# Packed transposes, a GpSimd cast and a hand-written order in an adapted linear layer

## The chip, the cores and the metric

The kernel runs on one core of a Trainium2 chip. The core has a matrix engine (TensorE, PE in the profile, its weight loads PEld), a vector engine (VectorE, DVE), a scalar engine (ScalarE, ACT), a general engine (GpSimd, POOL) and a synchronisation engine (SyncE, SP) that here only issues loads. All transfers run on the core's 16 DMA engines. The metric is device time in microseconds (us): the median of repeated runs. A profile comes from one profiled execution, whose own time is given beside its span.

## The reference

A linear layer whose weight is adapted by a low-rank product and normalised by column. x has 16 x 2048 rows of 256 values, all in fp32.

```python
W_adapted = W + scale * (lora_A @ lora_B)            # 256 x 256, rank 16
W_norm = np.sqrt(np.sum(W_adapted ** 2, axis=0, keepdims=True) + 1e-8)
W_final = (W_adapted / W_norm) * m                   # m: one value for each column
y = x.reshape(-1, 256) @ W_final                     # 32768 x 256
```

## The kernel before

**Start.** W, lora_A, lora_B and m are loaded (L60 to L66), and a short chain computes `w_final`, the final weight in bf16, as two halves of 128 input rows (index `c` or `kc`; input row k = 128 c + p lies on partition p). The chain is: transpose lora_A (L86), broadcast m with a matmul (L91), the low-rank product (L97), the sum with W (L106), squares (L110), column sums by a matmul with ones (L115), square root (L119), reciprocal (L124), and the scaling (L126).

**Main loop.** x is worked through in 8 blocks of 4096 rows. A block is one load of 4 MB on SP's queue (L52), in which partition p receives 32 consecutive rows of 256 values. Five buffers hold blocks, so the sixth load waits until the first block's store has emptied its buffer. A block is cut into 8 chunks of 4 rows for each partition, that is 512 rows, and 64 chunks make up the whole. For each chunk:

- TensorE transposes eight 128x128 pieces in fp32 (L141) into a PSUM tile `xt_ps`, which takes two banks; there are two such tiles.
- VectorE copies the tile to SBUF as bf16, `xt_sb` (L147); there are six such buffers.
- TensorE multiplies (L152): eight matmuls, each with one 128x128 piece of `xt_sb` as the stationary operand and a half of `w_final`, 256 columns, as the moving one, into `y_ps` (two banks, two tiles).
- ScalarE copies `y_ps` back over the rows of x in the block's buffer (L159).

After the last chunk ScalarE's queue issues the block's store of 4 MB (L161), and the buffer is free once it has landed. Loads are on one DMA queue (q1) and stores on the other (q10); both use the same 16 engines.

**Order.** The order on each engine is chosen by a planner from the program's order and its own costs; the start chain has a raised priority (L80). In the profile a number of transposes of later chunks are seen between the matmuls of earlier ones.

Of the kernel before, what the change touches and what calls it, by code (L numbers as in the profile page):

```python
# [10 lines left out]
@with_exitstack  # L11
def kernel(
    ctx: ExitStack,
    tc: tile.TileContext,
    x: bass.AP,
    W: bass.AP,
    lora_A: bass.AP,
    lora_B: bass.AP,
    m: bass.AP,
    scale: float,  # L20
    out: bass.AP,
):
    nc = tc.nc
    P = 128
    FP32 = mybir.dt.float32
    BF16 = mybir.dt.bfloat16
    AF = mybir.ActivationFunctionType
    ALU = mybir.AluOpType

    x_flat = x.flatten_outer_dims()  # L30
    out_flat = out.flatten_outer_dims()
    N, IN = x_flat.shape
    OUT = W.shape[1]
    R = lora_A.shape[1]
    KC = IN // P
    J = 4
    DJ = 32
    BLK = DJ * P
    NBLK = N // BLK

    assert IN == OUT and IN % P == 0 and OUT % P == 0 and N % BLK == 0

    consts = ctx.enter_context(tc.tile_pool(name="consts", bufs=1))
    startup = ctx.enter_context(tc.tile_pool(name="startup", bufs=1))
    xpool = ctx.enter_context(tc.tile_pool(name="xpool", bufs=5))
    xtpool = ctx.enter_context(tc.tile_pool(name="xtpool", bufs=6))
    pp_xt = ctx.enter_context(tc.tile_pool(name="pp_xt", bufs=2, space=bass.MemoryType.PSUM))
    pp_y = ctx.enter_context(tc.tile_pool(name="pp_y", bufs=2, space=bass.MemoryType.PSUM))

    def load_x(b):  # L50
        t = xpool.tile([P, DJ, IN], FP32, name="x_sb", tag="x_sb")
        nc.sync.dma_start(  # L52
            out=t,
            in_=x_flat[b * BLK : (b + 1) * BLK].rearrange("(p j) k -> p j k", p=P),
        )
        return t


    a_nat = startup.tile([P, KC, R], FP32)
    nc.scalar.dma_start(out=a_nat, in_=lora_A.rearrange("(c p) r -> p c r", p=P))  # L60
    w_nat = startup.tile([P, KC, OUT], FP32)
    nc.sync.dma_start(out=w_nat, in_=W.rearrange("(c p) o -> p c o", p=P))
    b_nat = startup.tile([R, OUT], FP32)
    nc.scalar.dma_start(out=b_nat, in_=lora_B)  # L64
    m_row = startup.tile([1, OUT], FP32)
    nc.scalar.dma_start(out=m_row, in_=m[None, :])  # L66

    identity = consts.tile([P, P], FP32)
    make_identity(nc, identity)
    ones = consts.tile([P, P], FP32)  # L70
    nc.vector.memset(ones, 1.0)
    eps_col = startup.tile([P, 1], FP32)
    nc.vector.memset(eps_col, 1e-8)

    warm = startup.tile([P, 1], FP32)
    nc.scalar.activation(out=warm, in_=eps_col, func=AF.Sqrt)  # L76

    w_final = consts.tile([P, KC, OUT], BF16)

    with tc.high_priority():  # L80
        b_bf = startup.tile([R, OUT], BF16)
        nc.vector.tensor_copy(out=b_bf, in_=b_nat)  # L82

        aT_ps = pp_y.tile([R, KC * P], FP32, tag="psy", name="aT_ps")
        for c in range(KC):
            nc.tensor.transpose(aT_ps[:, c * P : (c + 1) * P], a_nat[:, c, :], identity)  # L86
        aT = startup.tile([R, KC * P], BF16)
        nc.vector.tensor_copy(out=aT, in_=aT_ps)

        mb_ps = pp_y.tile([P, OUT], FP32, tag="psy", name="mb_ps")  # L90
        nc.tensor.matmul(mb_ps, ones[0:1, :], m_row, start=True, stop=True)  # L91
        m_all = startup.tile([P, OUT], FP32)
        nc.vector.tensor_copy(out=m_all, in_=mb_ps)  # L93

        ab_ps = pp_y.tile([P, KC, OUT], FP32, tag="psy", name="ab_ps")
        for c in range(KC):
            nc.tensor.matmul(  # L97
                ab_ps[:, c, :],
                aT[:, c * P : (c + 1) * P],
                b_bf,  # L100
                start=True,
                stop=True,
            )

        wa = startup.tile([P, KC, OUT], FP32)
        nc.vector.scalar_tensor_tensor(  # L106
            out=wa, in0=ab_ps, scalar=float(scale), in1=w_nat, op0=ALU.mult, op1=ALU.add
        )
        sq = startup.tile([P, KC, OUT], FP32)
        nc.vector.tensor_mul(out=sq, in0=wa, in1=wa)  # L110


        n2_ps = pp_y.tile([P, OUT], FP32, tag="psy", name="n2_ps")
        for c in range(KC):
            nc.tensor.matmul(  # L115
                n2_ps, ones, sq[:, c, :], start=(c == 0), stop=(c == KC - 1)
            )
        norm = startup.tile([P, OUT], FP32)
        nc.scalar.activation(out=norm, in_=n2_ps, func=AF.Sqrt, bias=eps_col)  # L119
        wam = startup.tile([P, KC, OUT], FP32)  # L120
        for c in range(KC):
            nc.vector.tensor_mul(out=wam[:, c], in0=wa[:, c], in1=m_all)  # L122
        rnorm = startup.tile([P, OUT], FP32)
        nc.vector.reciprocal(out=rnorm, in_=norm)  # L124
        for c in range(KC):
            nc.vector.tensor_mul(out=w_final[:, c], in0=wam[:, c], in1=rnorm)  # L126

    j_order = []
    for a in range(J // 2):
        j_order.append(a)  # L130
        j_order.append(a + J // 2)

    for b in range(NBLK):
        x_sb = load_x(b)


        for c in range(DJ // J):
            xt_ps = pp_xt.tile([P, KC, J * P], FP32, tag="psxt", name="xt_ps")
            for j in range(J):
                for kc in range(KC):  # L140
                    nc.tensor.transpose(  # L141
                        xt_ps[:, kc, j * P : (j + 1) * P],
                        x_sb[:, c * J + j, kc * P : (kc + 1) * P],
                        identity,
                    )
            xt_sb = xtpool.tile([P, KC, J * P], BF16, name="xt_sb")
            nc.vector.tensor_copy(out=xt_sb, in_=xt_ps)  # L147

            y_ps = pp_y.tile([P, J, OUT], FP32, tag="psy", name="y_ps")
            for kc in range(KC):  # L150
                for j in j_order:
                    nc.tensor.matmul(  # L152
                        y_ps[:, j, :],
                        xt_sb[:, kc, j * P : (j + 1) * P],
                        w_final[:, kc, :],
                        start=(kc == 0 and (j % (J // 2)) == 0),
                        stop=(kc == KC - 1 and (j % (J // 2)) == (J // 2) - 1),
                    )
            nc.scalar.copy(out=x_sb[:, c * J : (c + 1) * J, :], in_=y_ps)  # L159

        nc.scalar.dma_start(  # L161
            out=out_flat[b * BLK : (b + 1) * BLK].rearrange("(p j) k -> p j k", p=P),
            in_=x_sb,
        )


# [33 lines left out]
```

## Time and profile before

| | us |
|---|---|
| median of 11 runs (166.6 to 169.64) | 167.29 |
| profiled execution | 167.39 |
| its span, first to last instruction | 165.6 |
| TensorE matmul busy / weight loads | 129.3 / 108.2 |
| VectorE busy | 81.2 |
| ScalarE busy | 65.6 |
| GpSimd busy | 0.7 |
| block 0 lands | 13.9 |
| first store issued | 34.02 |
| last store issued | 153.39 |

67.55 MB are moved, at a mean of 408 GB/s over the span. The mean granted clock of TensorE is 0.973 of full speed.

How to read the lines: in the table of slices each digit is the busy share of a fortieth of the span in tenths. A group line gives the source line, the engine, the operation, output and input tiles with their shapes, the number of instructions, then busy us and the mean ns of one, then the idle time of the engine just before them and what ended most of it. Matmuls are pipelined, so the mean duration of one is longer than the spacing between two. The rows of stretches give, for a window of the span, each engine's busy time with its number of instructions, then the granted clock, the share of DMA and GB/s.

### The profile page before, as it was taken

To read this page: it belongs to the slowest core of one execution; us is meant where nothing else is said; L and a number is where in the kernel's file an instruction comes from. 1 tells how busy PE (TensorE), PEld (TensorE's weight loads), DVE (VectorE), ACT (ScalarE), POOL (GpSimd) and SP (SyncE) were. 2 spreads that over 40 slices of the span, in tenths; PEclk is the share of its full clock that TensorE was granted. 3 is DMA by queue.
4 is the path that set the end of the run, shared out by engine and by line. 5 is a ranking of instruction groups with operands and counts; after the bars stand their busy time and mean duration, and the time that the engine had idled before them with its cause. 6 is when DMAs were issued, how large, how long until landed. Compare 5 with 4: busy or idle time off the path is not lost.

```text
span 165.6 us, 2364 instructions
## 1 busy us (share of the span) xinstructions
PE 129.3 (78%) x1034; PEld 108.2 (65%) x1034; DVE 81.2 (49%) x76; ACT 65.6 (40%) x67; POOL 0.7 (0%) x6
## 2 busy tenths in 40 slices
PE   0149788888999889988998999889998699797000
PEld 0028677776788768876877778777786678685000
DVE  0155655558850895059553951577519350780000
ACT  3001244442068405960097039620780089329000
POOL 1000000000000000000000000000000000000000
PEclk9999999999999999999999999999999999999955
DMA  6999999999998999999999998999999999991885
GB/s 194 416 475 388 491 388 423 451 388 380 435 447 380 483 404 463 421 404 467 400 459 412 435 447 380 491 398 455 427 396 475 396 455 419 451 435 75 380 380 253
DMA packets 2892, 67.55 MB, mean 408 GB/s; under 512 B 561, under 2 KB 834, under 8 KB 834
## 3 DMA queue, kind: packets, MB, share of 16 engines
q1 hardware_dynamic: 1424, 33.82, 48.3%
q10 hardware_dynamic: 1458, 33.59, 47.3%
q8 instruction: 8, 0.13, 0.3%
q14 instruction: 2, 0.02, 0.0%
HBM read 33.85 MB, written 33.55 MB: 407 GB/s over the span
## 4 chain that ended last, share of the span: by engine, by line
PE 57%; DVE 22%; ACT 6%; DMA 4%; issue 2%; ACTq 1%
PE y_ps L152 32%; PE xt_ps L141 23%; DVE xt_sb L147 20%; ACT x_sb L159 6%; DMA m_row<-in_m_dram 4%; PE n_ps L115 1%; DVE rnorm L124 1%; PE mb_ps L91 1%; DVE w_final L126 0%; DVE sq L110 0%; DVE wa L106 0%; ACTq L60 0%; ACTq L64 0%; ACT norm L119 0%; PE ab_ps L97 0%
## 5 line engine op out<-in xcount | busy, mean ns | idle before, releaser
L147 DVE CAST xt_sb<-xt_ps 128x1024 bf16<-128x1024 f32 x64 | 75.5, 1219 | 55.8 <-PE xt_ps L141 41.8
L159 ACT COPY x_sb<-y_ps 128x1024 f32<-128x1024 f32 x64 | 63.6, 1014 | 75.2 <-PE y_ps L152 72.9
L141 PE MATMUL xt_ps<-identity,x_sb 128*128 128x128 f32 x512 | 71.3, 280 | 7.1 <-DVE xt_sb L147 6.5
L152 PE MATMUL y_ps<-w_final,xt_sb 128*128 128x256 bf16 x512 | 64.7, 272 | 6.1 <-DVE xt_sb L147 4.3
L141 PEld LDWEIGHTS xt_ps<-identity,x_sb 128*128 128x128 f32 x512 | 57.9, 143 | 15.9 <-DVE xt_sb L147 14.8
L152 PEld LDWEIGHTS <-xt_sb 128*128 128x128 bf16 x512 | 49.2, 97 | 16.7 <-DVE xt_sb L147 6.2
L119 ACT ACTIVATE norm<-n_ps,eps_col 128x256 f32<-128x256 f32 x1 | 0.5, 474 | 10.3 <-PE n_ps L115 10.3
L91 PE MATMUL mb_ps<-m_row,ones 1*128 1x256 f32 x2 | 1.2, 696 | 4.3 <-DMA m_row<-in_m_dram 4.3
L86 PE MATMUL aT_ps<-identity,a_nat 128*16 128x128 f32 x2 | 0.6, 394 | 4.0 <-DMA a_nat<-in_lora_A_dram 4.0
L91 PEld LDWEIGHTS mb_ps<-m_row,ones 1*128 1x128 f32 x2 | 0.5, 308 | 4.8 <-issue 4.8
L115 PE MATMUL n_ps<-sq,ones 128*128 128x256 f32 x4 | 2.1, 674 | 1.5 <-DVE sq L110 1.5
L82 DVE CAST b_bf<-b_nat 16x256 bf16<-16x256 f32 x1 | 0.3, 280 | 5.6 <-DMA b_nat<-in_lora_B_dram 5.6
L124 DVE RECIPROCAL rnorm<-norm 128x256 f32<-128x256 f32 x1 | 1.8, 1753 | 2.0 <-ACT norm L119 2.0
L86 PEld LDWEIGHTS aT_ps<-identity,a_nat 128*16 128x16 f32 x2 | 0.1, 88 | 4.0 <-issue 4.0
L115 PEld LDWEIGHTS n_ps<-sq,ones 128*128 128x128 f32 x4 | 1.2, 323 | 2.2 <-DVE sq L110 2.0
L76 ACT ACT_TABLE_LOAD x1 | 1.3, 1283 | 2.3 <-issue 2.3
L93 DVE COPY m_all<-mb_ps 128x256 f32<-128x256 f32 x1 | 0.4, 425 | 2.9 <-PE mb_ps L91 2.9
L126 DVE TENSOR_TENSOR w_final<-wam,rnorm 128x256 bf16<-128x256 f32 x2 | 0.8, 422 | 0.0
L122 DVE TENSOR_TENSOR wam<-wa,m_all 128x256 f32<-128x256 f32 x2 | 0.8, 416 | 0.0
L110 DVE TENSOR_TENSOR sq<-wa 128x512 f32<-128x512 f32 x1 | 0.7, 691 | 0.0
L106 DVE SCALAR_TENSOR_TENSOR wa<-ab_ps,w_nat 128x512 f32<-128x512 f32 x1 | 0.7, 691 | 0.0
L97 PE MATMUL ab_ps<-b_bf,aT 16*128 16x256 bf16 x2 | 0.6, 416 | 0.0
(11 smaller groups left out, 2.0 us busy)
## 6 DMA issues: line engine op xcount, KB each, us to landing
x_sb<-in_x_dram SPq DMA_DIRECT2D x8, 4096.0 KB, 31.3
out_dram<-x_sb ACTq DMA_DIRECT2D x8, 4096.0 KB, 25.7
w_nat<-in_W_dram SPq DMA_DIRECT2D x1, 256.0 KB, 3.0
a_nat<-in_lora_A_dram ACTq DMA_DIRECT2D x1, 16.0 KB, 3.1
b_nat<-in_lora_B_dram ACTq DMA_DIRECT2D x1, 16.0 KB, 5.3
m_row<-in_m_dram ACTq DMA_DIRECT2D x1, 1.0 KB
```

The source lines that it names most:

```text
L76: nc.scalar.activation(out=warm, in_=eps_col, func=AF.Sqrt)
L86: nc.tensor.transpose(aT_ps[:, c * P : (c + 1) * P], a_nat[:, c, :], identity)
L91: nc.tensor.matmul(mb_ps, ones[0:1, :], m_row, start=True, stop=True)
L106: nc.vector.scalar_tensor_tensor(out=wa, in0=ab_ps, scalar=float(scale), in1=w_nat, op0=ALU.mult, op1=ALU.add)
L115: nc.tensor.matmul(n2_ps, ones, sq[:, c, :], start=(c == 0), stop=(c == KC - 1))
L122: nc.vector.tensor_mul(out=wam[:, c], in0=wa[:, c], in1=m_all)
L124: nc.vector.reciprocal(out=rnorm, in_=norm)
L126: nc.vector.tensor_mul(out=w_final[:, c], in0=wam[:, c], in1=rnorm)
L141: nc.tensor.transpose(xt_ps[:, kc, j * P : (j + 1) * P], x_sb[:, c * J + j, kc * P : (kc + 1) * P], identity,)
L147: nc.vector.tensor_copy(out=xt_sb, in_=xt_ps)
L152: nc.tensor.matmul(y_ps[:, j, :], xt_sb[:, kc, j * P : (j + 1) * P], w_final[:, kc, :], start=(kc == 0 and (j % (J // 2)) == 0), stop=(kc ...
L159: nc.scalar.copy(out=x_sb[:, c * J : (c + 1) * J, :], in_=y_ps)
```

## The change

Four things change together.

1. **What is transposed.** GpSimd first casts a chunk of x to bf16 (`xb`, three buffers). Two neighbouring bf16 values of a row make up one 4-byte word, which is handed to TensorE as if it were one fp32 value. A row of 256 values is 128 words, so four transposes cover a chunk instead of eight. Partition p of the result holds input rows 2p and 2p+1 next to each other, for each of the 512 rows.
2. **What follows from it.** VectorE's copy out of PSUM moves 512 words instead of casting 1024 values. The result `xt` has three buffers; its PSUM tile takes one bank, and there are four. The stationary operand of a matmul is now every second bf16 value of `xt`. W and lora_A are loaded so that partition p holds input rows 2p and 2p+1 (index `t`), which matches.
3. **Order.** The planner is turned off and instructions stay in written order. The first five loads are written ahead of the start chain, later ones after the store that frees their buffer. The broadcast of m is written after the square root. Each chunk's cast, transposes and copy are written ahead of the matmuls of the chunk before; at the end of a block it is the other way round.
4. **Names.** The two halves of the loop become functions.

The stores stay one of 4 MB for each block.

```diff
-    xpool = ctx.enter_context(tc.tile_pool(name="xpool", bufs=5))
-    xtpool = ctx.enter_context(tc.tile_pool(name="xtpool", bufs=6))
-    pp_xt = ctx.enter_context(tc.tile_pool(name="pp_xt", bufs=2, space=bass.MemoryType.PSUM))
+    xpool = ctx.enter_context(tc.tile_pool(name="xpool", bufs=XBUFS))
+    xbpool = ctx.enter_context(tc.tile_pool(name="xbpool", bufs=3))
+    xtpool = ctx.enter_context(tc.tile_pool(name="xtpool", bufs=3))
+    pp_xt = ctx.enter_context(tc.tile_pool(name="pp_xt", bufs=4, space=bass.MemoryType.PSUM))
     pp_y = ctx.enter_context(tc.tile_pool(name="pp_y", bufs=2, space=bass.MemoryType.PSUM))
+    ctx.enter_context(tc.manual_schedule())
...
-    nc.scalar.dma_start(out=a_nat, in_=lora_A.rearrange("(c p) r -> p c r", p=P))
+    nc.scalar.dma_start(out=a_nat, in_=lora_A.rearrange("(p t) r -> p t r", t=KC))
     w_nat = startup.tile([P, KC, OUT], FP32)
-    nc.sync.dma_start(out=w_nat, in_=W.rearrange("(c p) o -> p c o", p=P))
+    nc.sync.dma_start(out=w_nat, in_=W.rearrange("(p t) o -> p t o", t=KC))
...
+    for b in range(XBUFS):
+        load_x(b)
...
-        mb_ps = pp_y.tile([P, OUT], FP32, tag="psy", name="mb_ps")
-        nc.tensor.matmul(mb_ps, ones[0:1, :], m_row, start=True, stop=True)
-        m_all = startup.tile([P, OUT], FP32)
-        nc.vector.tensor_copy(out=m_all, in_=mb_ps)
...
+    nc.scalar.activation(out=norm, in_=n2_ps, func=AF.Sqrt, bias=eps_col)
+
+    mb_ps = pp_y.tile([P, OUT], FP32, tag="psy", name="mb_ps")
+    nc.tensor.matmul(mb_ps, ones[0:1, :], m_row, start=True, stop=True)
+    m_all = startup.tile([P, OUT], FP32)
+    nc.vector.tensor_copy(out=m_all, in_=mb_ps)
...
-            for j in range(J):
-                for kc in range(KC):
-                    nc.tensor.transpose(
-                        xt_ps[:, kc, j * P : (j + 1) * P],
-                        x_sb[:, c * J + j, kc * P : (kc + 1) * P],
-                        identity,
-                    )
-            xt_sb = xtpool.tile([P, KC, J * P], BF16, name="xt_sb")
-            nc.vector.tensor_copy(out=xt_sb, in_=xt_ps)
...
+    def transposed(g):
+        b, c = divmod(g, CH)
+        rows = x_tiles[b][:, c * J : (c + 1) * J, :]
+        xb = xbpool.tile([P, J, IN], BF16, name="xb")
+        nc.gpsimd.tensor_copy(out=xb, in_=rows)
+        xt_ps = pp_xt.tile([P, J * P], FP32, tag="psxt", name="xt_ps")
+        for j in range(J):
+            nc.tensor.transpose(
+                xt_ps[:, j * P : (j + 1) * P], xb[:, j, :].bitcast(FP32), identity
+            )
+        xt = xtpool.tile([P, J * P, KC], BF16, name="xt")
+        nc.vector.tensor_copy(
+            out=xt.rearrange("p r t -> p (r t)").bitcast(FP32), in_=xt_ps
         )
+        xts[g] = xt
+
+    def multiplied(g):
...
+                nc.tensor.matmul(
+                    y_ps[:, j, :],
+                    xt[:, j * P : (j + 1) * P, t],
+                    w_final[:, t, :],
...
+        nc.scalar.copy(out=x_tiles[b][:, c * J : (c + 1) * J, :], in_=y_ps)
+        if c == CH - 1:
+            nc.scalar.dma_start(
+                out=out_flat[b * BLK : (b + 1) * BLK].rearrange("(p j) k -> p j k", p=P),
+                in_=x_tiles[b],
+            )
+            if b + XBUFS < NBLK:
+                load_x(b + XBUFS)
+
+    transposed(0)
+    for g in range(NCH):
+        first = (g + 1) % CH == 0
+        if first:
+            multiplied(g)
+        if g + 1 < NCH:
+            transposed(g + 1)
+        if not first:
+            multiplied(g)
```

## The prediction

> **What bounds the kernel now.** I read the times first, then the table of 40 slices, the groups, the DMA issues, and last the stretches around the end. The kernel takes 167.29 us (median of 11); the profiled run took 167.39, of which the span is 165.6 and 1.79 lies around it. My sums are made for the span; 1.79 is added at the end.
>
> From the slices and the queue table of the page:
>
> ```profile
> PE   0149788888999889988998999889998699797000
> DMA  6999999999998999999999998999999999991885
> GB/s 194 416 475 388 491 388 423 451 388 380 435 447 380 483 404 463 421 404 467 400 459 412 435 447 380 491 398 455 427 396 475 396 455 419 451 435 75 380 380 253
> ...
> q1 hardware_dynamic: 1424, 33.82, 48.3%
> q10 hardware_dynamic: 1458, 33.59, 47.3%
> ```
>
> Two resources are nearly full at once. The DMA engines are busy 96% of the span (48.3 + 47.3); TensorE runs at eight to nine tenths from 18 us to 153. The one hole in DMA is slice 36 (75 GB/s). The groups say what one chunk (512 rows, 64 of them) costs:
>
> ```profile
> L147 DVE CAST xt_sb<-xt_ps 128x1024 bf16<-128x1024 f32 x64 | 75.5, 1219 | 55.8 <-PE xt_ps L141 41.8
> L159 ACT COPY x_sb<-y_ps 128x1024 f32<-128x1024 f32 x64 | 63.6, 1014 | 75.2 <-PE y_ps L152 72.9
> L141 PE MATMUL xt_ps<-identity,x_sb 128*128 128x128 f32 x512 | 71.3, 280 | 7.1 <-DVE xt_sb L147 6.5
> L152 PE MATMUL y_ps<-w_final,xt_sb 128*128 128x256 bf16 x512 | 64.7, 272 | 6.1 <-DVE xt_sb L147 4.3
> L141 PEld LDWEIGHTS xt_ps<-identity,x_sb 128*128 128x128 f32 x512 | 57.9, 143 | 15.9 <-DVE xt_sb L147 14.8
> L152 PEld LDWEIGHTS <-xt_sb 128*128 128x128 bf16 x512 | 49.2, 97 | 16.7 <-DVE xt_sb L147 6.2
> ```
>
> The first y matmul starts at 18.36 and the last copy out ends at 153.35, so a chunk takes (153.4 - 18.4)/64 = 2.11 us: 8 transposes and 8 matmuls, 0.89 and 0.87 to 1.05 us per set in the chain in order of time, plus hand-overs with VectorE's 1.22 us cast. The end, in stretches (columns: PE, PEld, DVE, ACT, POOL busy, granted clock, DMA share, GB/s):
>
> ```profile
> 149.00:150.00 1.00, 0.86 (x8) 0.78 (x8) 0.00 (x0) 1.00 (x2) 0.00 (x0) 1.00 0.54 229
> 150.00:151.00 1.00, 1.00 (x10) 0.78 (x9) 0.00 (x0) 0.79 (x2) 0.00 (x0) 1.00 0.14 49
> 151.00:152.00 1.00, 0.81 (x8) 0.65 (x7) 0.00 (x0) 1.00 (x2) 0.00 (x0) 1.00 0.08 33
> 152.00:154.00 2.00, 0.31 (x3) 0.03 (x1) 0.00 (x0) 1.15 (x2) 0.00 (x0) 1.00 0.00 0
> 154.00:155.00 1.00, 0.00 (x0) 0.00 (x0) 0.00 (x0) 0.00 (x0) 0.00 (x0) 1.00 1.21 524
> 155.00:160.00 5.00, 0.00 (x0) 0.00 (x0) 0.00 (x0) 0.00 (x0) 0.00 (x0) 0.66 0.98 419
> ```
>
> Here DMA has finished all stores but the last and waits for compute; the last store (S7) is issued at 153.39, lands 11.1 us later, and the span ends 12.2 us after its issue. So compute sets the end, by a small margin: it can win only the DMA hole, and no more.
>
> **The new chunk, engine by engine.** TensorE: 4 fp32 transposes instead of 8, 0.89/2 = 0.45 us, and the same 8 matmuls. Their stationary operand is now read with a step of 4 bytes, which no row shows. Below: unchanged, 0.87. Nearest row: the fp32 weight load, which also takes 128 words 4 bytes apart, 143 ns against 97; overlapped, that is 8 x 0.143 = 1.15. Above: not overlapped with the matmul of about 0.109 (0.87/8), 8 x 0.252 = 2.0. I take 1.0; TensorE then needs 1.45 us, 2.45 at worst.
>
> VectorE: a copy of 128x512 fp32 out of PSUM. By L147 (1024 wide, 1219 ns) and the copy L93 (256 wide, 425 ns) one element costs 1.034 ns, so 0.69 us instead of 1.22. ScalarE: unchanged, 1.01.
>
> GpSimd: a new cast of 128x1024 fp32 to bf16 per chunk, ahead of everything else. No row has it; the nearest are two of its own:
>
> ```profile
> 0.31 0.10 POOL L181 MEMSET const-bfloat16-1.0<- 128x1 bf16 x1
> ...
> 0.73 0.20 POOL masks.py:197 MEMSET identity<- 128x128 f32 x1 [0.29 <-POOLq L181]
> 1.01 0.29 POOL masks.py:199 TENSOR_SCALAR_AFFINE_SELECT identity<-identity 128x128 f32<-128x128 f32 x1
> ```
>
> A write alone costs (0.205 - 0.10)/127 = 0.83 ns per element, read-compute-write (0.294 - 0.10)/127 = 1.53. For 1024 elements: 0.95 and 1.67 us. **The rule against this**: the Trainium skill, "GPSIMD Engine Reference", section 3.1, measures about 2.6 cycles per element at 1.2 GHz for its two-input add, and advises VectorE for elementwise work; by that the cast takes an estimated 1024 x 2.6/1.2 = 2.2 us plus 0.1 = 2.3. The same section gives 1.03 cycles for a body of at most two operations, an estimated 0.98. The add's price comes from two operands sharing a read port, and a cast has one, so I take 1.3 us, between the two rows, and keep 0.95 and 2.3.
>
> So the period is 1.45 us, set by TensorE, with GpSimd next.
>
> **The schedule with DMA included.** Alone, a 4 MB load takes 9.7 us (block 0 landed at 13.9, block 1 at 23.6). With a store running each gets half: loads 3 and 4 landed at 52.1 and 71.5, 19.3 apart. From landing to the store's issue a block takes: cast 1.3, transposes 0.5, copy 0.69, matmuls 1.0, copy out 1.01, hand-overs 0.2, and 7 more chunks at 1.45: 14.9. **The clock** adds to it: the first 16 transposes, after idleness, took 3.29 us, against 2.22 for 16 at 93.40, and the clock row drops to 0.66 and 0.50 once TensorE stops. The skill's "TensorE: Matmul & The Clock Gate", Part 1, says that an idle window of about 3.4 us halves the clock until about 3.4 us of work. Before, TensorE never paused; now it works some 12 us of each 19 and starts most blocks cold. By the trace that costs about 1.1 us per block, by the rule up to 1.7; I take 1.7, so 16.6. If blocks were on the path, the last alone would pay it. The following shows why it is mostly covered.
>
> S0 is issued at 13.9 + 16.6 = 30.5 instead of 34.02 and moves from 31.2. Load 2 then has 2.1 of its 9.7 left, which take twice as long: 35.4. Then loads land every 19.3: L3 54.7, L4 74.0, L5 93.3, L6 112.6, L7 131.9. Stores land S0 50.5, S1 69.8, S2 89.1, S3 108.4, S4 127.7; S5 shares until 131.9 and ends at 139.5; S6 149.2. Loads 5 to 7, which wait on SP for S0 to S2 to free a buffer (50.5, 69.8, 89.1), are then still behind queued loads, so that wait costs nothing. Blocks 1 and 2 follow back to back (42.1, 53.7); later ones wait for their load. S7 is issued at 131.9 + 16.6 = 148.5, before S6 is through: no hole. A block time longer by d delays S0 by d and, because loads then run alone for longer, brings L7 forward by d. S7's issue hardly moves, until chunks run back to back from first to last: 13.9 + 4.7 + 64r = 149.2, so r = 2.04 us. **Any chunk period below about 2.0 us gives the same end**, that of DMA.
>
> **The sum.** Up to 145 us the DMA moved 61.3 MB (stretches, GB/s by time). The other 6.24 MB at 428 GB/s, the mean of 5 to 145, take 14.6: 159.6, and 2.4 us later (last bytes about 163.2, end 165.6) the span ends at 162.0. If instead the slowest engine decides, it was done with S6 at about 151.5; 9.2 for S7 (154.1 to 163.3) and 2.4 give 163.1. I take 162.5: the hole of 3.1 us is what is won. Plus 1.79 is 164.3; the median lies 0.1 below the profiled run: **164.2 us**.
>
> Edits with one answer. mb_ps moved behind the norm and the contiguous layout of W and lora_A: w_final comes at about 16.3 instead of 17.16, while chunk 0 is ready at about 16.4; a gain of nothing, or 0.9 lost at block 0 if the cover goes, which L7 gives back. All five first loads are issued as before (SP: 1.2 to 4.7). Three xt buffers instead of six: at most two are in flight in the written order. PSUM stays at eight banks, the y buffers at two. The hand-written order queues each chunk's transposes ahead of the chunk before's matmuls on TensorE, so a late cast holds matmuls up; it costs something only if GpSimd is the slowest. ACT issues the store in its old place (0.34 us).
>
> **Rivals.** (a) *DMA sets the end*: 164.2, between 162.8 (mixed traffic at 435 GB/s instead of 428) and 165.3 (slowest engine): 0.74. (b) *Partial gain*: a period of 2.0 to 2.08, or a late S7 that leaves 1 to 3 us of hole: 165.3 to 166.8: 0.04. (c) *Hole only moved* (ends within 166.8 to 167.8): 0.04. (d) *GpSimd becomes the bound*, slower: at r = 2.3 the end is 13.9 + 5.8 + 63 x 2.32 + 12.2 = 178.1, plus 1.79 about 180. It decides from a cast of about 2.08 us, 2.4 cycles per element; for it speaks the two-input price, against it both GpSimd rows: 0.13. (e) *Strided weight loads don't overlap*: TensorE at 2.45 gives about 13.9 + 4.7 + 64 x 2.45 + 14 = 189; against it, fp32 weight loads and their moves overlap today (8 pairs in 0.89, 0.111 each): 0.05.
>
> **Numbers.** Changes under 0.3% (0.5 us) can't be told from none. Faster is (a) and (b), 0.78; same (c), 0.04; slower (d) and (e), 0.18. The range holds (a) to (c) and the lower edge of (d), a cast of 2.1 us: 162.8 to 169.0. The likeliest case alone has 162.8 to 165.3.
>
> **What would show it.** DMA at nine tenths with no hole near slice 36; S7 issued near 148 while S6 is still moving; transposes x256; GpSimd casts under 2 us; VectorE copies near 0.69; TensorE waiting for x loads with rests between blocks. Wrong if casts start every 2.1 us or more, if the matmuls of a chunk take over 1.6 us, or if DMA's rate falls with earlier stores.

## The result, and the profile after

The changed kernel is faster, by less than half of what was forecast: the ratio to the kernel before is 0.9917, with a 95% interval of 0.9894 to 0.994, or 1.4 us of 167.29. Four of its 12 executions (168.3 to 170.84 us) were slow ones and are left out of the ratio; the other eight have a median of 165.84 us, all 12 one of 166.47. Measured a second time, later (run 10), the same kernel took 164.85 us, a ratio of 0.9862 (0.9832 to 0.9892). The forecast was 164.2 us, a gain of 3.1; the change is worth 1.4 to 2.3.

The page of the changed kernel, the lines that answer to those shown of before (slices, then DMA queues, then groups):

```profile
PE   0264799999997699008995099901999039980000
DMA  6998999999999999999999999999999999999992
...
q1 hardware_dynamic: 1296, 33.82, 49.3%
q10 hardware_dynamic: 1330, 33.59, 47.8%
q8 instruction: 6, 0.10, 0.2%
q14 instruction: 3, 0.02, 0.0%
...
L148 POOL CAST xb<-x_sb 128x1024 bf16<-128x1024 f32 x64 | 65.3, 1046 | 75.6 <-DMA x_sb<-in_x_dram 61.4
L174 ACT COPY x_sb<-y_ps 128x1024 f32<-128x1024 f32 x64 | 64.3, 1012 | 71.5 <-PE y_ps L166 39.5
L166 PE MATMUL y_ps<-w_final,xt 128*128 128x256 bf16 x512 | 71.5, 288 | 1.6 <-DVE xt L155 1.6
L155 DVE COPY xt<-xt_ps 128x512 f32<-128x512 f32 x64 | 43.9, 690 | 84.4 <-PE xt_ps L151 84.4
L151 PE MATMUL xt_ps<-identity,xb 128*128 128x128 f32 x256 | 44.2, 306 | 34.0 <-POOL xb L148 34.0
L166 PEld LDWEIGHTS <-xt 128*128 128x128 bf16 x512 | 51.5, 103 | 12.1 <-DVE xt L155 4.8
```

The hole of slice 36 (counted from 0) is gone and DMA is full until the last slice. TensorE now rests between blocks, and GpSimd's largest wait is for loads of x. The chain that ended last, 57% TensorE and 22% VectorE before, is 52% DMA:

```profile
DMA 52%; PE 29%; DVE 5%; ACT 2%; issue 1%; POOL 1%; ACTq 0%; POOLq 0%; SPq 0%
```

The end in stretches, with the columns used before (busy by engine, granted clock, DMA share, GB/s):

```profile
146.00:147.00 1.00, 0.77 (x8) 0.44 (x5) 0.00 (x0) 1.00 (x2) 0.00 (x0) 1.00 0.99 426
147.00:148.00 1.00, 0.00 (x0) 0.00 (x0) 0.00 (x0) 0.87 (x1) 0.00 (x0) 1.00 0.99 426
...
158.00:160.00 2.00, 0.00 (x0) 0.00 (x0) 0.00 (x0) 0.00 (x0) 0.00 (x0) 0.50 0.84 360
160.00:161.00 1.00, 0.00 (x0) 0.00 (x0) 0.00 (x0) 0.00 (x0) 0.00 (x0) 0.50 0.46 197
161.00:162.00 1.00, 0.00 (x0) 0.00 (x0) 0.00 (x0) 0.00 (x0) 0.00 (x0) 0.50 0.08 33
```

The last store (S7) is issued at 147.91 and DMA doesn't stop for it. But its share sinks step by step from 158 to 162: some engines are done while others still work. That is where the missing gain went. The trace makes it countable: each 4 MB transfer leaves 16 completion marks, as many as there are DMA engines, and I read them as one of each. First and last mark in us:

| | S6 | S7 | S7, last minus first |
|---|---|---|---|
| before | 150.1, 152.9 | 164.3, 164.5 | 0.2 |
| changed | 149.9, 153.0 | 159.6, 162.6 | 3.0 |

Before, S7 was issued after all engines had stopped, and its marks lie 0.2 us apart. In the changed kernel the engines go on from S6 to S7 without a stop, and the lag is still there. The first mark of S7 is 4.7 us earlier than before and the last, which sets the end, 1.9.

### The profile page after: what moved, and what is told of

Same layout as the page of the kernel before. It is cut to its first block, busy times and chain, and to the rows that moved or that the text cites. A ratio compares the mean times of both kernels' runs of the same rounds, so it can differ in the third digit from the quotient of the medians.

```text
span 163.7 us, 2032 instructions
## 1 busy us (share of the span) xinstructions
PE 102.8 (63%) x778; PEld 85.8 (52%) x778; DVE 50.7 (31%) x76; ACT 66.3 (41%) x67; POOL 66.0 (40%) x70
## 4 chain that ended last, share of the span: by engine, by line
DMA 52%; PE 29%; DVE 5%; ACT 2%; issue 1%; POOL 1%; ACTq 0%; POOLq 0%; SPq 0%
DMA out_dram<-x_sb 27%; DMA x_sb<-in_x_dram 22%; PE y_ps L166 18%; PE xt_ps L151 9%; DMA b_nat<-in_lora_B_dram 3%; ACT x_sb L174 2%; PE n_ps L118 1%; DVE xt L155 1%; DVE w_final L132 1%; DVE rnorm L130 1%; PE mb_ps L123 1%; POOL xb L148 1%; DVE wam L128 0%; DVE sq L113 0%; DVE wa L109 0%
## 5 line engine op out<-in xcount | busy, mean ns | idle before, releaser
L148 POOL CAST xb<-x_sb 128x1024 bf16<-128x1024 f32 x64 | 65.3, 1046 | 75.6 <-DMA x_sb<-in_x_dram 61.4
L174 ACT COPY x_sb<-y_ps 128x1024 f32<-128x1024 f32 x64 | 64.3, 1012 | 71.5 <-PE y_ps L166 39.5
L166 PE MATMUL y_ps<-w_final,xt 128*128 128x256 bf16 x512 | 71.5, 288 | 1.6 <-DVE xt L155 1.6
L155 DVE COPY xt<-xt_ps 128x512 f32<-128x512 f32 x64 | 43.9, 690 | 84.4 <-PE xt_ps L151 84.4
L151 PE MATMUL xt_ps<-identity,xb 128*128 128x128 f32 x256 | 44.2, 306 | 34.0 <-POOL xb L148 34.0
L166 PEld LDWEIGHTS <-xt 128*128 128x128 bf16 x512 | 51.5, 103 | 12.1 <-DVE xt L155 4.8
L151 PEld LDWEIGHTS xt_ps<-identity,xb 128*128 128x128 f32 x256 | 33.8, 158 | 38.6 <-POOL xb L148 37.7
L132 DVE TENSOR_TENSOR w_final<-wam,rnorm 128x256 bf16<-128x256 f32 x2 | 1.8, 922 | 0.0
```

Of the source, the lines that this page charges most:

```text
L132: nc.vector.tensor_mul(out=w_final[:, t], in0=wam[:, t], in1=rnorm)
L148: nc.gpsimd.tensor_copy(out=xb, in_=rows)
L151: nc.tensor.transpose(xt_ps[:, j * P : (j + 1) * P], xb[:, j, :].bitcast(FP32), identity)
L155: nc.vector.tensor_copy(out=xt.rearrange("p r t -> p (r t)").bitcast(FP32), in_=xt_ps)
L166: nc.tensor.matmul(y_ps[:, j, :], xt[:, j * P : (j + 1) * P, t], w_final[:, t, :], start=(t == 0 and (j % (J // 2)) == 0), stop=(t == KC - ...
L174: nc.scalar.copy(out=x_tiles[b][:, c * J : (c + 1) * J, :], in_=y_ps)
```

## The experiments

The theory after the traces: compute has slack, DMA sets the end, and of the 16 DMA engines the slowest. The rivals: (A) the chunk's time still counts in the end; (B) the engines' own traffic in SBUF slows the transfers; (C) the lag comes of sharing the engines between two queues, or of stores. The ratio is always to the kernel before on the same chip.

**1. The transfers alone.**

```diff
     for b in range(XBUFS):
         load_x(b)
+    for b in range(NBLK):
+        nc.scalar.dma_start(
+            out=out_flat[b * BLK : (b + 1) * BLK].rearrange("(p j) k -> p j k", p=P),
+            in_=x_tiles[b],
+        )
+        if b + XBUFS < NBLK:
+            load_x(b + XBUFS)
...
-    transposed(0)
```

> All compute is left out (and the loads of m, lora_A, lora_B and W stay): a block is stored again as soon as it has landed, with the changed kernel's two DMA queues and five buffers, so the output is x. Theory (the slowest of the 16 DMA engines, about 3 us behind the fastest once loads and stores share them, sets the end; compute has slack): 163 to 166 us, within 1% of the changed kernel's 165.8, and the 16 completion marks of the last store 2 to 4 us apart. Rival A (compute still sets part of the end: chunk period, cold TensorE blocks): at least 2 us faster than the changed kernel. Rival B (GpSimd's and the other engines' traffic in SBUF slows the transfers): the mean DMA rate rises from 427 to 432 GB/s or more and the end comes 1.5 to 2 us earlier.

Measured: 162.35 us, ratio 0.9725 (0.9698 to 0.9752). S7's marks are 159.2 and 159.7, 0.5 us apart, as all along the run. The theory's expectation failed and the rivals' came true, at first sight. But the fastest engine ends where the fastest of the changed kernel ends (159.2 against 159.6): what compute adds is the lag of the others. And in this run loads and stores share the engines from 18.5 us on (the first large packet of the stores' queue) without drifting apart, which speaks against (C).

**2. The old transposes in the new order.** Without GpSimd's cast, with eight fp32 transposes straight from x:

```diff
-        xb = xbpool.tile([P, J, IN], BF16, name="xb")
-        nc.gpsimd.tensor_copy(out=xb, in_=rows)
...
+            for kc in range(KC):
+                nc.tensor.transpose(
+                    xt_ps[:, kc, j * P : (j + 1) * P],
+                    x_tiles[b][:, c * J + j, kc * P : (kc + 1) * P],
+                    identity,
+                )
...
+        nc.vector.tensor_copy(out=xt, in_=xt_ps)
```

> The changed kernel's order, with the old transposes: eight fp32 transposes of a chunk straight from x, the old cast on VectorE, no GpSimd cast, two PSUM tiles of two banks. Theory: the chunk period is about 0.89 + 0.87 = 1.8 us on TensorE, below 2.0, so DMA sets the end and the time is the changed kernel's, 165.3 to 166.3 (ratio to before 0.988 to 0.994): the order gave the gain and the packing nothing of its own. Rival A (the chunk period counts): 1.8 lies 60% of the way from 1.31 to 2.11, so about 166.7, ratio 0.997. If the period is still 2.0 or more, as the hand-over to VectorE's 1.22 us cast would make it: 167 or more.

Measured: 165.18 us, ratio 0.9901 (0.9875 to 0.9927), the changed kernel's time. The stores S0 to S4 are issued at 32.96 to 93.81, four blocks in 60.85 us, so a chunk takes 1.90 us: slower than the 1.31 of the packed kernel, faster than the 2.11 of before, and below 2.04. The written order, with the new start that goes with it, brings the whole gain without the packing.

**3. Two casts for each chunk.**

```diff
         nc.gpsimd.tensor_copy(out=xb, in_=rows)
+        nc.gpsimd.tensor_copy(out=xb, in_=rows)
```

> The changed kernel with each GpSimd cast done twice: 2 x 1.046 = 2.09 us of GpSimd for each chunk, just past the break-even of 2.04. Theory: blocks run back to back behind GpSimd, the last store is issued at about 13.9 + 5.5 + 63 x 2.09 = 151 to 152 instead of 147.9, still before or just at the end of the store before it on the slowest engine (152.9); time 165.8 to 167. Rival A (every chunk's time is on the path): 64 x 0.78 us of added period would give over 200. Rival B (GpSimd's traffic slows DMA): the mean DMA rate between 60 and 145 us falls below 425 GB/s.

Measured: 165.42 us, ratio 0.9906 (0.9879 to 0.9934). The chunk takes 2.09 us (S0 at 34.60, S7 at 151.83: 117.23/56), 60% more than in the changed kernel, and the time is the same. Rival A falls in its form that every chunk's time counts. But here the hole is back: S7 is issued when most engines have finished S6 (marks 149.6 to 152.2).

```profile
150.00:155.00 5.00, 0.70 (x7) 0.38 (x4) 0.00 (x0) 1.80 (x2) 0.00 (x0) 0.92 0.51 216
```

All engines then end S7 together, at 162.8 to 163.0. If S7 takes each of them 9.7 us, the fastest stood still for an estimated 3.5 us and the slowest for 1. A hole in which mostly those engines wait that are ahead costs the end little. DMA ran at 431 GB/s between 60 and 145 us, as in the changed kernel's run 10, so B's first sign is missing.

**4. Past the break-even.** As above, with a further cast of half a chunk.

> The changed kernel with two and a half casts for each chunk on GpSimd: 2.09 + about 0.57 = 2.66 us, clearly past the break-even of 2.04. Theory: GpSimd sets the end by the prediction's formula, 13.9 + 6.1 + 63 x 2.66 + 12.2 + 1.8 = 201 to 202. If DMA waits and casts only add in part: below 190.

Measured: 208.41 us in both executions, ratio 1.2465 (1.2416 to 1.2514). The period is 2.76 instead of 2.66 (S0 at 39.60, S7 at 194.41), which is the difference: 0.1 x 63 = 6.6 us. Of the periods run, 2.76 us counts at every chunk, while 1.31, 1.90 (run 2) and 2.09 (run 3) can't be told apart in the time (165.2 to 165.8 us).

**5. One queue for loads and stores.**

```diff
-            nc.scalar.dma_start(
+            nc.sync.dma_start(
                 out=out_flat[b * BLK : (b + 1) * BLK].rearrange("(p j) k -> p j k", p=P),
                 in_=x_tiles[b],
             )
-            if b + XBUFS < NBLK:
-                load_x(b + XBUFS)
+            if b >= 1 and b - 1 + XBUFS < NBLK:
+                load_x(b - 1 + XBUFS)
```

> The changed kernel with the stores issued from SP, on the loads' queue, in the order S0 S1 L5 S2 L6 S3 L7 S4 to S7, so that each DMA engine does loads and stores one after the other and never shares between two queues. Theory: the engines stay together as during the first loads (marks 0.5 us apart), so the end comes up to 3 us earlier: 163 to 164.5, ratio 0.975 to 0.983. Rival C (an engine is slow in itself, or the spread comes of stores as such): marks 2 to 4 us apart and the time of the changed kernel or above, 165.8 to 168. Holes of DMA where a load waits for a store on SP would show as slices below nine tenths.

Measured: 165.41 us, ratio 0.9898 (0.9875 to 0.9921). S7's marks are 3.3 us apart. The engines drift apart without any sharing, so the expected mechanism, and rival C's sharing with it, is wrong. The marks of the single transfers show how it begins. Load 2 ends with 15 engines within 0.4 us of each other and one 1.9 us late; load 3 is the same, in load 4 (marks 52.7 to 55.4) two engines are over 2.3 late, and in the first store (62.5 to 65.1) three are, by 1.7 or more. Just before load 2's end, at 30.1 us, the trace has a packet of the queue called instruction in its list: 16 KB, 1.03 us long. The changed kernel shows the same: a first fetch at 31.2 (1.07 us), and load 2's marks are 0.0 to 0.6 for 15 engines and 1.7 for one. TensorE's 778 pairs of weight load and matmul are 1556 instructions, and at six packets of 16 KB (98 KB) that makes about 64 bytes each: I read this as its instruction stream, fetched through the same 16 engines while they are full.

**6. Many instructions that touch no x.** The transfers alone, plus a stream of matmuls on constants:

```diff
+    for i in range(1536):
+        nc.tensor.matmul(fill_ps[:, :P], ones_bf, ones_bf, start=True, stop=True)
```

> The transfers alone, as in the run without compute, plus 1536 matmuls of 128 columns on constants, which read no x and write nothing that is stored (the output is x). They fill TensorE's instruction stream, which the trace shows being fetched in packets of 16 KB through the same DMA engines. Theory (each fetch holds up one of the 16 DMA engines by 1 to 2 us while all are full, and the slowest engine sets the end): 6 to 12 such fetches, completion marks of the last store 2 to 4 us apart instead of 0.5, and 1.5 to 4 us more than the 162.35 of the transfers alone: 164 to 166.5. Rival B (it is the engines' traffic on x in SBUF): marks stay 0.5 us apart and the time 162.2 to 162.8.

Measured: 166.03 us, ratio 0.9943 (0.9912 to 0.9975), 3.7 more than the transfers alone (on another chip; the two ratios give 3.6). TensorE is done by 90 us, and no block waits for it:

```profile
q1 hardware_dynamic: 1296, 33.82, 48.8%
q10 hardware_dynamic: 1330, 33.59, 47.8%
q8 instruction: 12, 0.20, 0.5%
...
L83 PE MATMUL fill_ps<-ones_bf 128*128 128x128 bf16 x1536 | 88.0, 221 | 1.0 <-DVE ones_bf L80 1.0
```

Twelve fetches of 1.0 to 1.1 us, and marks up to 4.4 us apart in the loads, 3.3 in the stores and 2.5 in the last.

**7. Traffic in SBUF, few instructions.** Twice: first with 65 to 200 instructions on each engine, and then, since that run left the question open, with fewer than 60.

> The transfers alone plus heavy traffic in SBUF with few instructions: some 110 GpSimd casts and VectorE copies, 64 ScalarE copies and 100 matmuls of 512 columns, all on constants (the output is x). No engine has more than about 250 instructions. Theory (instruction fetches): at most a fetch or two, marks below 1.5 us apart, 162.2 to 163.3. Rival B (traffic in SBUF slows transfers): marks 2 us or more apart, or a lower mean rate, 164 or more.

Measured: 164.86 us, 1.6 above the expected top. One 16 KB fetch (at 24.1) and three of 8 KB fell into the span; the first transfer to land after the first of them (load 1, 30.3 to 32.1) ends with one engine at 1.7 and all others within 0.6, and a lag of this size stays to the end (S7: 1.8). Load 0 landed at 14.1 to 14.6 with its marks 0.6 apart, although TensorE, VectorE, ScalarE and GpSimd had been at work since about 2.5 us. One fetch costs more than I gave it, or traffic takes part.

This order holds in nearly every trace, and the fetch comes at very different times. The first 16 KB fetch is at 11.1 us in run 6, 24.1 here, 31.2 in the changed kernel and 39.5 in run 4; the first load with one late engine is load 0, 1, 2 and 3, and every load before it is at most 0.7 us apart. In 11 of the 12 traces with such fetches the first transfer to land after the first of them has one engine 1.1 to 1.5 us behind the other fifteen. The twelfth is run 3, where several engines are apart by then. The three traces without one (run 1, its repeat and the second form below) never show more than 0.7 in a 4 MB transfer.

The second form, and beside it the transfers alone:

```diff
+    for i in range(55):
+        nc.gpsimd.tensor_copy(out=p_out, in_=src)
+        nc.vector.tensor_mul(out=v_out, in0=src, in1=src)
     for b in range(NBLK):
+        for i in range(5):
+            nc.scalar.copy(out=a_out, in_=src)
         nc.scalar.dma_start(
```

> The transfers alone plus heavy traffic in SBUF from fewer than 60 instructions on each engine: 55 GpSimd casts and 55 VectorE products of 2048 elements, 40 ScalarE copies of 2048, no TensorE (the output is x). Theory (instruction fetches, not traffic, set the engines apart): no fetch inside the span, marks of the last store at most 0.7 us apart, the time of the transfers alone within 0.5 us. Rival B (traffic in SBUF slows transfers): 164 or more, as in the run with 100 to 200 instructions on each engine.

> The transfers alone once more, beside the next run on the same chip (no compute; the output is x). 162.2 to 162.9, marks of the last store 0.5 us apart, no instruction fetch inside the span.

The transfers alone took 163.07 us on this chip. The traffic run took 220.47, because GpSimd and VectorE needed that long for their own filler; what counts is its transfers:

```profile
DMA  7999999999999999999999999999920000000000
...
q1 hardware_dynamic: 1296, 33.82, 37.3%
q10 hardware_dynamic: 1330, 33.59, 35.6%
...
L85 POOL CAST p_out<-src 128x2048 bf16<-128x2048 f32 x55 | 210.9, 3835 | 6.0 <-DVE src L80 2.6
L86 DVE TENSOR_TENSOR v_out<-src 128x2048 f32<-128x2048 f32 x55 | 210.7, 3831 | 1.9
```

No instruction row stands among the queues. Its last store landed at 161.5 with marks 0.6 us apart, against 160.5 and 0.3 alone: later by 0.9, more than the 0.5 that I had allowed. Of the 0.9, 0.6 are there at the first load (15.4 against 14.8). From 30 to 145 us DMA ran at 433 GB/s, while GpSimd and VectorE were busy all but without a pause (columns: DVE, ACT and POOL busy, clock, DMA share, GB/s):

```profile
30.00:145.00 115.00, 113.99 (x30) 56.94 (x30) 113.11 (x31) 1.00 1.00 433
```

Rival B falls: traffic doesn't set the engines apart. TensorE did nothing in this run. That its work alone could set them apart is spoken against by the first form, whose load 0 ends together beside a busy TensorE, and by the order of first fetch and first late engine.

**8. More fetches in the real kernel.**

```diff
+        for i in range(8):
+            nc.tensor.matmul(xt_ps[:, :32], ones_bf, ones_bf[:, :32], start=True, stop=True)
         for j in range(J):
             nc.tensor.transpose(
```

> The changed kernel with 8 further small matmuls (32 columns, on constants, overwritten by the transposes) in each chunk: 512 more pairs, so about 10 fetches of 16 KB instead of 6. The chunk period rises by some 0.5 us to 1.8, below 2.0. Theory: the slowest engine is hit once more or not at all, marks of the last store 3 to 5 us apart, time 0 to 2 us above the changed kernel's 165.8 or the 165.2 to 165.4 of the other runs. If fetches don't matter: unchanged. Above 168: the period went past 2.0.

Measured: 166.49 us, ratio 0.9943 (0.9924 to 0.9962), with 10 fetches. S6's marks are 4.7 us apart. S7 is issued at 149.79, just late enough for the engines that had finished S6 to wait a little, and ends with 3.0. The median is above the changed kernel's, but the intervals of the two ratios overlap (0.9924 to 0.9962 and 0.9894 to 0.994) and its two measurements differ more than that. The run decides nothing.

**9. The packing without the written order.**

```diff
-    ctx.enter_context(tc.manual_schedule())
```

> The changed kernel with the planner left on: the packed transposes and the GpSimd cast without the hand-written order. Theory: any order with a chunk period below 2.0 us gives the same end, and 4 transposes in place of 8 give at most 2.11 - 0.45 = 1.66: 165 to 166, ratio 0.987 to 0.993, equal to the changed kernel and to the old transposes in the new order. Rival (the order is what helps): at or above 166.7, ratio 0.997 or more.

Measured: 167.87 us, ratio 1.001 (0.9979 to 1.0041): no gain. My expectation was wrong, and TensorE's list around the seventh block's end says why (start, length, instruction, idle before and releaser):

```profile
122.14 1.47 PE L150 MATMUL xt_ps<-identity,xb 128*128 128x128 f32 x12
123.97 0.66 PE L150 MATMUL xt_ps<-identity,xb 128*128 128x128 f32 x4 [0.36 <-POOL xb L147]
124.96 0.65 PE L150 MATMUL xt_ps<-identity,xb 128*128 128x128 f32 x4 [0.33 <-POOL xb L147]
131.11 1.12 PE L150 MATMUL xt_ps<-identity,xb 128*128 128x128 f32 x4 [5.49 <-POOL xb L147]
132.01 5.28 PE L165 MATMUL y_ps<-w_final,xt 128*128 128x256 bf16 x24
```

The planner puts the next block's first transposes (131.11) ahead of the matmuls of this block's last six chunks, 48 in all; the 24 of the last line are the first three chunks'. The transposes wait 5.49 us for a block that hasn't landed, and the finished block's matmuls wait behind them. S6 goes out at 141.78 instead of 127.83, S7 at 153.00 instead of 147.91, and DMA has holes in the last quarter (253 and 269 GB/s in slices 34 and 36, counted from 0).

**10. The exception at a block's end, and the changed kernel again.**

```diff
-        first = (g + 1) % CH == 0
+        first = g + 1 == NCH
```

> The changed kernel once more, on the same chip as the next runs. Theory: 165.4 to 166.5, ratio 0.988 to 0.996, completion marks of the last store 2.5 to 4 us apart, six fetches of 16 KB.

> The changed kernel without the exception at a block's end: the next block's first cast, transposes and copy are always written ahead of the last chunk's matmuls, so that these wait on TensorE until the next block has landed. Stores then go out about 4 us after the next load's landing: the seventh (S6) at some 132.4 + 4 = 136.5 instead of 127.8. Theory: the store queue still holds earlier stores until about 140 to 143, so DMA has no hole and the time is the changed kernel's, 165.4 to 166.5. Rival (the written exception is what the planned order lacks): S6 late enough to open a hole, 167 or more, as with the planner on.

Measured: the changed kernel 164.85 us, ratio 0.9862 (0.9832 to 0.9892), with S7's marks 2.2 us apart and a span of 162.5; without the exception 164.88, ratio 0.9862 (0.9835 to 0.9888). So one chunk's matmuls behind the next block's transposes cost nothing measurable, and the matmuls of six chunks (run 9) cost the gain. That the stores still queued on DMA cover the one is likely, but not shown by a trace: the only profile without the exception is of an execution of 169.28 us. The repeat's first mark of S7 is 159.2, its last 161.4, and the span ends 1.1 us later. In the first profile the marks are 159.6 and 162.6, and the rest is also 1.1. So of the 1.2 us between the two spans, 0.8 is lag.

No version was found that beats the changed kernel clearly. The transfers alone, at 162.35 and 163.07, are the floor of this scheme of eight 4 MB blocks; the changed kernel is 1.8 us above it on one chip (164.85 against 163.07), and 3.5 in the first measurements (165.84 against 162.35).

## Why the prediction went wrong

**What bounds the kernel before**: right. Compute set the end by a small margin, and only DMA's hole could be won. Runs 2 and 4 bear it out from both sides of the break-even, and run 3 close to it.

**The new chunk**: right, with margins on the safe side. TensorE needs 0.44 + 0.87 = 1.31 us for a chunk (forecast 1.45). The strided weight load costs nothing (103 ns against 97; 1.0 us for the set was forecast, 0.87 measured), which settles rival (e). VectorE's copy is 690 ns, as worked out. The cast takes 1046 ns, between the two GpSimd rows and near the lower: (1046 - 100)/1024 x 1.2 = 1.11 cycles per element. This is an estimate with the 1.2 GHz of "GPSIMD Engine Reference", section 3.1. The 2.6 cycles there are for a two-input add, which no run here measures; they don't carry over to this cast, and the 1.03 of the same section lies nearer. That settles rival (d). (By the same sum the 2.08 us of (d) are 2.3 cycles and not the 2.4 given.)

**The schedule**: right within 0.6 us where it mattered. Forecast and measured: S0's issue 30.5 and 31.11, L7's landing 131.9 and 132.4, S7's issue 148.5 and 147.91. In between it was partly wrong: the first large packet of S0 moved 4.2 us after its issue and not 0.7, and S0 to S4 finished 2.9 to 4.0 us later than forecast even by their first marks (53.9 to 130.6 against 50.5 to 127.7). S5 and S6 came out within 0.7 again (first marks 140.2 and 149.9). That block time cancels between S0 and L7 held roughly (run 3: S0 is issued 3.5 later, L7 lands 5.3 earlier). The clock's price was about right. TensorE's rows of the changed kernel in the last block, and the stretches around them:

```profile
133.66 2.10 PE L151 MATMUL xt_ps<-identity,xb 128*128 128x128 f32 x8 [6.96 <-POOL xb L148]
135.56 1.91 PE L166 MATMUL y_ps<-w_final,xt 128*128 128x256 bf16 x8
137.26 1.06 PE L151 MATMUL xt_ps<-identity,xb 128*128 128x128 f32 x4
...
136.00:138.00 2.00, 2.00 (x11) 1.69 (x10) 0.49 (x1) 0.45 (x1) 1.55 (x2) 0.50 1.03 442
138.00:140.00 2.00, 2.00 (x19) 1.75 (x18) 0.95 (x2) 1.21 (x2) 1.21 (x2) 0.92 0.99 426
```

The granted clock is 0.50 until after 138, 4.7 us from the first transpose (133.66 to 138.33), where "TensorE: Matmul & The Clock Gate", Part 1, says about 3.4. By the starts of instructions four transposes take about 0.85 us instead of 0.44 and a set of matmuls 1.71 instead of 0.87. Part of that falls into a wait for the next cast, so the last block loses about 1.8 us, near the 1.7 that I took. From L7's landing to S7's issue the block took 15.5 us (forecast 16.6). It was hidden, as said.

**The sum**: here it failed, in its sentence "I take 162.5: the hole of 3.1 us is what is won". It put the end between that of the mean engine (162.0) and that of the slowest (163.1). A span ends with the slowest alone, and the profiled one ended at 163.7. The step before it had the same fault: "S6 149.2" is near the time when the fastest engine is done (149.9); the slowest was at 153.0. Of the hole the slowest engine could win only what it had itself stood still: before, 11.6 us from the last mark of S6 to the last of S7, now 9.7. So it won 1.9 of the 3.1 us.

The prediction's own sum for the slowest engine, 163.1, was also 0.6 short: that engine ended S6 at 152.9 in the trace of before and not at 151.5, its S7 came 9.7 later in the changed kernel and not 9.2, and the span ended 1.1 us after its last mark and not 2.4: 152.9 + 9.7 + 1.1 = 163.7. It read the ends from rows of stretches, which lie over a microsecond before the marks (S7 of before: 163.3 and 164.5), and the errors nearly cancel; that 163.1 came so near is luck. Half of the miss in the span (0.6 of 1.2) is thus the choice of 162.5, half this term. As a time, 163.1 plus 1.79 less 0.1 is 164.8 and not the 165.3 given for this case; the second measurement was 164.85. The prediction saw the slow engine in the trace but not its cause. The 1.9 us are those of the profiled pair; the medians gain 1.4 and 2.3, and the spread of S7's marks differs likewise (3.0 and 2.2 us).

**The rivals**: (a) happened in kind, but 1.6 us above its number (165.84 against 164.2) and above the 165.3 that I gave as its own upper end; the second measurement, 164.85, lies below that end. None of the slower cases came true.

**Shown and not shown.** Shown: a stream of instructions that touches no x, with its fetches, is enough to set the engines apart (run 6), SBUF traffic is not (run 7), sharing between queues is not needed (run 5), and the first late engine comes with the first fetch, early or late (run 7). No run takes the fetches out of the real kernel, so that all of its lag comes from them is argued. Only argued, too: how one fetch of 1 us leaves an engine 1.1 to 1.9 us late, and why the lags of all engines together (measured from the first mark, 25.6 us in the changed kernel's S7 against 3.3 in the transfers alone) exceed the fetches' own 6.8 us. That stays open.

## What to carry to other kernels

Where compute and transfers are nearly level, first work out the break-even period. Here it was an estimated 2.04 us a chunk: below it, faster compute was worth nothing in the runs made, and a written order that only removed hand-over waits (1.90) gained as much as it did together with halved transposes (1.31). Sum a transfer-bound end by the slowest DMA engine and not by bytes over mean rate: look at the spread of the last transfers' completion marks, and at whether an idle hole had let the engines catch up. Don't let an engine wait for the next block while several finished chunks stand behind it (six in run 9 cost the gain).

## What the runs showed of the hardware

- Packets of the queue called instruction run on the 16 DMA engines: 16 KB at a time, with a number that goes with TensorE's instructions (6 fetches for 778 weight-load and matmul pairs, 8 for the 1034 of before, 10 for 1290, 12 for 1536), about 1 us each. In 11 of 12 traces the first one leaves one engine 1.1 to 1.5 us behind. While DMA is full it doesn't catch up (run 7, first form: 1.7 to 1.8 from 30 us to the end).
- At the start the clock row can't be relied on: in the changed kernel it shows 1.00 from 18 to 22 us, while the first two sets of matmuls take 1.89 and 1.65 us instead of 0.87. Later rests are shown as they are (0.50 from 132 to 138).
- A GpSimd cast of 2048 elements and a VectorE product with two SBUF inputs took 3.83 us each when run side by side. From the 1046 ns for 1024 elements the cast alone would take an estimated 2.0, and VectorE's 691 and 416 ns for 512 and 256 elements give its product an estimated 2.3. Together they took about nine tenths of the sum (4.3). That is close to taking turns, as "SBUF — State Buffer", section "SBUF: two separate sides", says of the port pair that the two share; neither was measured alone. The changed kernel's VectorE copies read PSUM, and its cast took 1046 ns beside them (1040 in run 4).
